# A conditioned decoder block: the gate, attention and state-space projections with tokens on the partitions and 512 weight columns moving

## The chip, the cores and the metric

The kernel runs on one core of one Trainium2 chip. The core has five engines with instruction streams of their own: TensorE (PE), VectorE (DVE), ScalarE (ACT), GpSimd (POOL) and SyncE (SP), which issues the large loads. The metric is the device time of one execution in microseconds.

## The reference

One decoder block for 256 tokens of width 2048, in float32. An input projection `h @ w_in` of the normed, conditioned input gives the state-space input u (1024 columns), q, k and v (1024 each) and two gates (2048 each). Attention and a state-space branch run beside each other and are merged under the gates:

```python
attn = moba_attention(q, k, v, rel_bias)          # 8 heads of 128, causal
ssm = s5_branch(u, ...)                           # scan over tokens, gelu, then y * sigmoid(y @ w_glu + b)
m = sigmoid(gate_a) * (ssm @ w_proj_ssm) + sigmoid(gate_b) * (attn @ w_proj_attn)
x = x + mod * (m @ w_out)
x = x + mod * (squared_relu(h2 @ w_ff1) @ w_ff2)  # d_ff = 8192, then a last norm
```

The modulations come from c through `w_ada`. (The names in this excerpt are shortened.)

## The kernel before, in words

All weights stream once through the core as 439 units of 128x1024 (512 KB). For each unit SP issues a load into `wraw` (seven buffers), ACT casts it to `whi` (L144), DVE forms the rest `wlo = wraw - whi` (L146), and PE multiplies: three products make one product in nearly full precision (activation high times weight high, low times high, high times low). `whi` and `wlo` have four buffers each.

Two forms of multiplication use a unit. `gemm_t` (lines 188 to 190) holds a 128x128 block of the weights still and moves 256 tokens of the activations: 24 matmuls of 256 columns, and the result has output features on partitions and tokens along the row. `gemm_n` (lines 315, 317, 319) holds a 128x128 block of the activations still and moves 512 columns of the weights: 12 matmuls, and the result has tokens on partitions and features along the row. Both write four PSUM banks of 128x512, one accumulation over all k-tiles of the contraction.

In the order of the program: the first units of the input projection, among them ten k-tiles of the first gate columns; the other input units, with six more gate k-tiles; three runs of 16 gate units (i = 1, 2, 3), with attention and then the scan of the state-space branch beside them; `proj_attn` in two halves of eight units (columns cg 0 and 1) with the eight units of `w_glu` between; `proj_ssm` in two halves; `w_out` in two halves; the two MLP products. Before, the gates, `proj_attn`, `w_glu` and `proj_ssm` use `gemm_t`; v, `w_out` and the MLP's first product use `gemm_n`.

Work beside the stream is emitted in lanes: a lane is a list of jobs with a rate, and after each unit `step` adds the rate to a credit and emits jobs while the credit is at least one; `flush` emits what is left. The attention jobs are in lane "m" with rate 1.5, and from the middle of run i=1 that lane holds the scan's jobs `bgl` with rate 0.43. Lane "ada" holds jobs that multiply and reduce a modulation's weights on DVE (L374); they share the `wraw` buffers. A scheduler then sorts each engine's instructions by its own priorities, so the emitted order is not the final one.

The gates live in `ga` (slot X16; x is loaded into the same slot later) and `gb` (slot S1). The merge is in the loop over cg at lines 1188 to 1195: gate times projection (L1193, which also undoes a permutation of the tokens by four), plus the attention part (L1194), and a split of the sum into `mh` and `ml` for `w_out`. Attention keeps scratch rows `asc` in a part of `ga` that is not yet written by the gates. `vr`, `vi` and `ys` are the small matmuls on both sides of the scan.

## Time and profile before

| what | value |
|---|---|
| median of 3 runs | 1403.4 us (1403.07 to 1407.36) |
| the profiled execution, first to last instruction | 1403.3 us |
| PE busy, matmuls | 1369.2 us, 9282 |
| DVE busy, instructions | 1040.4 us, 1474 |
| ACT busy, instructions | 737.7 us, 1004 |
| POOL busy, instructions | 40.9 us, 94 |
| read from HBM | 347.27 MB, 249 GB/s over the span |
| granted TensorE clock, mean | 0.996 |

Busy time of an engine is the union of its instructions' times; matmuls overlap one another, so a matmul's printed duration is longer than the distance between two starts. The chain that ended last is followed back from the last instruction to what released each step. A group's row gives line, engine, operation, output and inputs, count, busy us and mean ns of one, and the idle time ahead with what ended it.

### The profile page before, as it was taken

The numbers are of one execution on the slowest core, as the hardware profiler recorded it, in microseconds if no ns is written. First come the engines' busy times: TensorE is split into PE (matmuls) and PEld (weight loads), VectorE is DVE, ScalarE is ACT, GpSimd is POOL, SyncE is SP. The second block draws the span as 40 slices with busy tenths as digits, with TensorE's granted clock in tenths as the row PEclk, the third lists the DMA queues.
The fourth block names the chain that finished last, engine by engine and source line by source line (L and its number), as shares of the span: only waits on it lengthen the run. The fifth ranks groups of instructions, "written<-read, shape, count | busy, mean of one in ns | idle before, by whom it ended". The sixth has DMA issues, their size and how long they took to land.

```text
span 1403.3 us, 23470 instructions
## 1 busy us (share of the span) xinstructions
PE 1369.2 (98%) x9282; PEld 1219.2 (87%) x9282; DVE 1040.4 (74%) x1474; ACT 737.7 (53%) x1004; POOL 40.9 (3%) x94
## 2 busy tenths in 40 slices
PE   7889999999999999999999999999999999999997
PEld 5779899989999999988888888888888888888885
DVE  5788899776898888977777775777676555554676
ACT  4464565577545853446555554544463553635543
POOL 1000000410001300000000000000000000000000
PEclk9999999999999999999999999999999999999998
DMA  9999996885567988887588777778777566565551
GB/s 352 361 395 332 336 324 221 231 272 205 175 212 236 314 325 301 301 332 291 175 300 282 216 244 246 242 251 276 250 249 235 192 195 190 186 194 187 181 204 60
DMA packets 113293, 353.19 MB, mean 252 GB/s; under 512 B 12080, under 2 KB 12096, under 8 KB 113056
## 3 DMA queue, kind: packets, MB, share of 16 engines
q1 hardware_dynamic: 110096, 346.61, 72.1%
q0 software_dynamic: 2800, 4.58, 1.3%
q8 instruction: 72, 1.18, 0.3%
q10 hardware_dynamic: 288, 0.52, 0.1%
q14 instruction: 37, 0.30, 0.1%
HBM read 347.27 MB, written 2.29 MB: 249 GB/s over the span
## 4 chain that ended last, share of the span: by engine, by line
PE 86%; DMA 7%; DVE 4%; ACT 2%; issue 1%; DVEq 0%; SPq 0%; ACTq 0%
PE pw L216 15%; PE pn L315 9%; PE pn L317 9%; PE pn L319 9%; PE pt L188 8%; PE pt L190 8%; PE pt L189 8%; PE pw L218 8%; DMA wraw<-in_w_in_dram 5%; DVE wlo L146 2%; PE pn L246 2%; PE pn L247 2%; PE pn L248 2%; DVE wraw L374 1%; ACT whi L144 1%
## 5 line engine op out<-in xcount | busy, mean ns | idle before, releaser
L146 DVE TENSOR_TENSOR wlo<-wraw,whi 128x1024 fp32r<-128x1024 f32 x439 | 535.8, 1223 | 276.6 <-ACT whi L144 275.3
L144 ACT CAST whi<-wraw 128x1024 fp32r<-128x1024 f32 x439 | 460.5, 1051 | 531.7 <-PE pn L317 167.8
L216 PE MATMUL pw<-mh,whi 128*128 128x512 f32 x896 | 314.5, 397 | 0.0
L188 PE MATMUL pt<-ah,whi 128*128 128x256 f32 x896 | 251.9, 288 | 5.9 <-ACT whi L144 3.8
L189 PE MATMUL pt<-ah,whi 128*128 128x256 f32 x896 | 249.5, 284 | 0.0
L218 PE MATMUL pw<-mh,wlo 128*128 128x256 f32 x896 | 249.2, 281 | 0.0
L190 PE MATMUL pt<-ah,wlo 128*128 128x256 f32 x896 | 239.7, 286 | 1.4 <-DVE wlo L146 1.1
L374 DVE SCALAR_TENSOR_TENSOR wraw<-wraw,cb 128x1024 f32<-128x1024 f32 x176 | 213.5, 1219 | 0.0
L216 PEld LDWEIGHTS pw<-mh,whi 128*128 128x128 f32 x896 | 167.9, 188 | 39.5
L317 PE MATMUL pn<-whi,ff 128*128 128x512 f32 x480 | 187.0, 390 | 0.0
L315 PE MATMUL pn<-whi,ff 128*128 128x512 f32 x480 | 186.9, 389 | 0.0
L319 PE MATMUL pn<-wlo,ff 128*128 128x512 f32 x480 | 185.8, 389 | 0.0
L188 PEld LDWEIGHTS pt<-ah,whi 128*128 128x128 f32 x896 | 171.6, 192 | 10.3 <-ACT whi L144 5.4
L189 PEld LDWEIGHTS pt<-ah,whi 128*128 128x128 f32 x896 | 172.1, 192 | 0.4 <-DVE ah L146 0.2
L218 PEld LDWEIGHTS pw<-mh,wlo 128*128 128x128 f32 x896 | 169.1, 189 | 1.0
L190 PEld LDWEIGHTS pt<-ah,wlo 128*128 128x128 f32 x896 | 165.0, 192 | 3.8 <-DVE wlo L146 3.4
L315 PEld LDWEIGHTS pn<-whi,ff 128*128 128x128 f32 x480 | 90.1, 188 | 19.0
L319 PEld LDWEIGHTS pn<-wlo,ff 128*128 128x128 f32 x480 | 90.1, 188 | 18.7
L317 PEld LDWEIGHTS pn<-whi,ff 128*128 128x128 f32 x480 | 90.1, 188 | 18.5
L1354 DVE TENSOR_TENSOR y<-y,pn 128x512 f32<-128x512 f32 x48 | 31.0, 684 | 14.6 <-PE pn L319 14.6
L315 PE MATMUL pn<-whi,mh 128*128 128x512 f32 x96 | 37.7, 393 | 1.7 <-ACT whi L144 1.7
L317 PE MATMUL pn<-whi,mh 128*128 128x512 f32 x96 | 37.4, 389 | 0.0
(422 smaller groups left out, 1737.4 us busy)
## 6 DMA issues: line engine op xcount, KB each, us to landing
wraw<-in_w_ff_dram SPq DMA_DIRECT2D x256, 512.0 KB, 4.3
wraw<-in_wat_dram SPq DMA_DIRECT2D x176, 512.0 KB, 5.7
wraw<-in_w_in_dram SPq DMA_DIRECT2D x128, 512.0 KB, 5.5
wraw<-in_w_out_dram SPq DMA_DIRECT2D x32, 512.0 KB, 6.3
wraw<-in_wan_dram SPq DMA_DIRECT2D x16, 512.0 KB, 8.7
wraw<-in_w_proj_attn_dram SPq DMA_DIRECT2D x16, 512.0 KB, 6.5
wraw<-in_w_proj_ssm_dram SPq DMA_DIRECT2D x16, 512.0 KB, 6.7
wraw<-in_w_glu_dram SPq DMA_DIRECT2D x8, 512.0 KB, 5.7
```

The source lines that it names most:

```text
L144: h = self.nc.scalar.copy(hi, src)
L146: s = self.nc.vector.tensor_sub(lo, src, hi.bitcast(F32))
L188: nc.tensor.matmul(o, hi[:, c], xh[:, kx, :], start=st, stop=False, skip_group_check=True)
L189: nc.tensor.matmul(o, hi[:, c], xl[:, kx, :], start=False, stop=False, skip_group_check=True)
L190: self.mm = nc.tensor.matmul(o, lo[:, c], xh[:, kx, :], start=False, stop=sp, skip_group_check=True)
L216: nc.tensor.matmul(banks[b], hi[:, c], x2[:, k0 + k].rearrange("p h s -> p (h s)"), start=i + k == 0, stop=False, skip_group_check=True)
L218: self.mm = nc.tensor.matmul(banks[b][:, 0:S], lo[:, c], x2[:, k0 + k, 0, :], start=False, stop=i == n - 1 and k == 1, skip_group_check=True)
L315: nc.tensor.matmul(o, xh[:, kx, tk], hi[:, c], start=q == 0 and not seeds, stop=False, skip_group_check=bool(seeds))
L317: nc.tensor.matmul(o, xl[:, kx, tk], hi[:, c], start=False, stop=False, skip_group_check=bool(seeds))
L319: self.mm = last = nc.tensor.matmul(o, xh[:, kx, tk], lo[:, c], start=False, stop=q == n - 1, skip_group_check=bool(seeds))
L374: v.scalar_tensor_tensor(w, w, 1.0, self.cb[:, (i % 2) * 1024:(i % 2 + 1) * 1024], op0=OP.mult, op1=OP.mult, accum_out=pc[:, i:i + 1])
L1354: v.tensor_add(d, d, banks[b])
```

## The change

The 96 units of the gates, `proj_attn` and `proj_ssm` go from `gemm_t` to `gemm_n`; `w_glu` stays. `gemm_n` gets the hook `mid` that `gemm_t` had. `ga`, `gb` and the partial gate `gp` now hold tokens on partitions, [P, half of the columns, half of the tokens, 1024], and attention's scratch is the second half of `ga`, columns 0 to 767. The tokens' permutation is now undone where the gated state-space output `gg` is split (the view `nat`), so the multiply of the merge is plain. The contraction of `w_out` needs features on partitions, so the merged rows are transposed on PE: `merged`, eight jobs of four 128x128 transposes into one PSUM tile `trm`, in a lane "tr" of rate 0.75 that starts at credit -1. The jobs of cg 0 run beside the units of `proj_ssm` cg 1, those of cg 1 beside the first half of the units of `w_out`'s first half. The split into `mh` and `ml` then reads PSUM.

```diff
@@ -294,12 +294,14 @@
             then.append((o, c))
         yield then
 
-    def gemm_n(self, src, kts, c0, xh, xl, koff=0, tail=1, seeds=None):
+    def gemm_n(self, src, kts, c0, xh, xl, koff=0, tail=1, seeds=None, mid=None):
         nc = self.nc
         banks = self.seeded("pn", seeds)
         n = len(kts)
         held, prev = [], None
         for i, unit in enumerate(self.stream(src, kts, c0)):
+            if mid and i == n // 2:
+                mid()
             u = (i,) + unit
             held.append(u)
             for t in range(2):
@@ -1024,11 +1026,11 @@
 
         def g_home(part):
             if part and "p" not in gpart:
-                gpart["p"] = self.slot("S4", [P, 8, S], name="gp")
+                gpart["p"] = self.slot("S4", [P, 2, 1024], name="gp")
             if not part:
-                self.ga = self.slot("X16", [P, KT, S], name="ga")
-            t = gpart["p"] if part else self.ga
-            return [(t[:, 2 * b:2 * b + 2, :], pair) for b in range(4)]
+                self.ga = self.slot("X16", [P, 2, 2, 1024], name="ga")
+            t = gpart["p"] if part else self.ga[:, 0]
+            return [(t[:, b // 2, (b % 2) * 512:(b % 2 + 1) * 512], lambda p: p) for b in range(4)]
 
         gpart = {}
 
@@ -1066,8 +1068,8 @@
             home = {0: lambda: qk_home(0), 1: lambda: qk_home(1), 2: v_home, 3: u_home, 4: lambda: g_home(True)}[which]
             old = home() if g0 else None
             c0 = (1024, 2048, 3072, 0, 4096)[which]
-            if which == 2:
-                banks = self.gemm_n(win, kts, c0, self.ah, self.al, seeds=old)
+            if which in (2, 4):
+                banks = self.gemm_n(win, kts, c0, self.ah, self.al, seeds=old, mid=mid)
             else:
                 banks = self.gemm_t(win, kts, c0, self.ah, self.al, mid=mid, seeds=old)
             evac(g_home(False) if which == 4 and g0 else home(), banks)
@@ -1107,9 +1109,9 @@
         qkvu(2, 2, 2)
         self.flush("tab")
         ga = self.ga
-        self.asc = ga[:, 8:14, :].rearrange("p k s -> p (k s)").rearrange("p (i n) -> p i n", i=2)
+        self.asc = ga[:, 1, :, 0:768]
         self.yatt = self.slot("T", [P, 8, S], name="yatt")
-        gb = self.slot("S1", [P, KT, S], name="gb")
+        gb = self.slot("S1", [P, 2, 2, 1024], name="gb")
         def scan(b):
             self.ssm_scan(b)
 
@@ -1139,15 +1141,14 @@
             if i == 3:
                 self.lanes["ada"][1] = RS2
             dst, c0 = ((ga, 4096), (ga, 5120), (gb, 6144), (gb, 7168))[i]
-            banks = self.gemm_t(win, range(KT), c0, self.ah, self.al, mid=to_ssm if i == 1 else None)
+            banks = self.gemm_n(win, range(KT), c0, self.ah, self.al, mid=to_ssm if i == 1 else None)
             for b in range(4):
-                nc.scalar.copy(dst[:, (i % 2) * 8 + 2 * b:(i % 2) * 8 + 2 * b + 2, :],
-                               banks[b].rearrange("p (k s) -> p k s", s=S))
+                nc.scalar.copy(dst[:, i % 2, b // 2, (b % 2) * 512:(b % 2 + 1) * 512], banks[b])
         self.flush("m")
         self.lanes["ada"][1] = RPA
 
         def sig(t, q):
-            d = t[:, 4 * q:4 * q + 4, :].rearrange("p k s -> p (k s)")
+            d = t[:, q // 2, q % 2]
             with self.after(self.done[-1][1]):
                 nc.scalar.activation(d, d, AF.Sigmoid)
 
@@ -1157,9 +1158,9 @@
         for k in range(4):
             self.split(yh[:, 2 * k:2 * k + 2], yl[:, 2 * k:2 * k + 2], self.yatt[:, 2 * k:2 * k + 2])
         def proj_attn(cg):
-            banks = self.gemm_t(a["w_proj_attn"][0], range(8), cg * 1024, yh, yl)
+            banks = self.gemm_n(a["w_proj_attn"][0], range(8), cg * 1024, yh, yl)
             for b in range(4):
-                d = gb[:, cg * 8 + 2 * b:cg * 8 + 2 * b + 2, :].rearrange("p k s -> p (k s)")
+                d = gb[:, cg, b // 2, (b % 2) * 512:(b % 2 + 1) * 512]
                 v.tensor_mul(d, d, banks[b])
 
         proj_attn(0)
@@ -1180,19 +1181,29 @@
                                      bias=self.bglu[:, 2 * b + k:2 * b + k + 1])
             s = slice(2 * b, 2 * b + 2)
             v.tensor_mul(sc4(t), sc4(t), yT[:, s])
-            self.split(gg[:, 0, s], gg[:, 1, s], t)
+            nat = lambda z: z.rearrange("p k (c s) -> p k s c", s=4)
+            self.split(nat(gg[:, 0, s]), nat(gg[:, 1, s]), sc4(t))
         proj_attn(1)
         self.a2("mh")
         mh, ml = self.ah, self.al
+        def merged(cg, t, c):
+            p = self.aux("trm")
+            for k in range(4):
+                nc.tensor.transpose(p[:, k * P:(k + 1) * P], ga[:, cg, t, c * 512 + k * P:c * 512 + (k + 1) * P],
+                                    self.ident)
+            ks, tk = slice(cg * 8 + 4 * c, cg * 8 + 4 * c + 4), slice(t * P, (t + 1) * P)
+            self.split(mh[:, ks, tk], ml[:, ks, tk], p.rearrange("p (k s) -> p k s", s=P))
+
         for cg in range(2):
-            banks = self.gemm_t(a["w_proj_ssm"][0], range(8), cg * 1024, gg[:, 0], gg[:, 1])
+            banks = self.gemm_n(a["w_proj_ssm"][0], range(8), cg * 1024, gg[:, 0], gg[:, 1])
             for b in range(4):
-                s = slice(cg * 8 + 2 * b, cg * 8 + 2 * b + 2)
-                d = ga[:, s, :]
-                dk = d.rearrange("p k (c s) -> p k s c", s=4)
-                v.tensor_mul(dk, dk, banks[b].rearrange("p (k s c) -> p k s c", k=2, s=4))
-                v.tensor_add(d, d, gb[:, s, :])
-                self.split(mh[:, s], ml[:, s], d)
+                c = slice((b % 2) * 512, (b % 2 + 1) * 512)
+                d = ga[:, cg, b // 2, c]
+                v.tensor_mul(d, d, banks[b])
+                v.tensor_add(d, d, gb[:, cg, b // 2, c])
+            if cg:
+                self.flush("tr")
+            self.lane("tr", [lambda cg=cg, t=t, c=c: merged(cg, t, c) for c in range(2) for t in range(2)], .75, -1.0)
         self.lane("x", self.load_x(), .25, -.5)
         self.lane("g1", [lambda ch=ch: g1_row(ch) for ch in range(4)], .25)
         self.lanes["ada"][1] = RWO
@@ -1208,7 +1219,7 @@
                                     turns=((), ((KT - 3, 1),)))
                 banks = next(parts)
             else:
-                banks = self.gemm_n(a["w_out"][0], range(KT), cg * 1024, mh, ml)
+                banks = self.gemm_n(a["w_out"][0], range(KT), cg * 1024, mh, ml, mid=lambda: self.flush("tr"))
             self.flush("x", "g1")
 
             def add1(t):
```

In the order of instructions three places show it. First PE, in gate run i=2. `ah` is the high part of the activations, `pt` and `pn` are the PSUM banks. Before, half a unit is:

```order
L188 MATMUL pt_4176<-ah,whi 128x256
L189 MATMUL pt_4176<-ah,whi 128x256
L190 MATMUL pt_4176<-ah,wlo 128x256
L188 MATMUL pt_4176<-ah,whi 128x256
L189 MATMUL pt_4176<-ah,whi 128x256
L190 MATMUL pt_4176<-ah,wlo 128x256
L188 MATMUL pt_4177<-ah,whi 128x256
L189 MATMUL pt_4177<-ah,whi 128x256
L190 MATMUL pt_4177<-ah,wlo 128x256
L188 MATMUL pt_4177<-ah,whi 128x256
L189 MATMUL pt_4177<-ah,whi 128x256
L190 MATMUL pt_4177<-ah,wlo 128x256
```

After, one whole unit is:

```order
L317 MATMUL pn_3790<-whi,ah 128x512
L319 MATMUL pn_3790<-whi,ah 128x512
L317 MATMUL pn_3791<-whi,ah 128x512
L319 MATMUL pn_3791<-whi,ah 128x512
L317 MATMUL pn_3792<-whi,ah 128x512
L319 MATMUL pn_3792<-whi,ah 128x512
L317 MATMUL pn_3793<-whi,ah 128x512
L319 MATMUL pn_3793<-whi,ah 128x512
L321 MATMUL pn_3790<-wlo,ah 128x512
L321 MATMUL pn_3791<-wlo,ah 128x512
L321 MATMUL pn_3792<-wlo,ah 128x512
L321 MATMUL pn_3793<-wlo,ah 128x512
```

A unit has half as many matmuls, each twice as wide, and in this unit all four that read `wlo` stand behind the eight that read `whi`; before, each third matmul reads `wlo`.

Second DVE, beside the same run i=2, where the scan's rows are (`rw`, `sri`, `tbl`: the scan's rows, its output and its table of powers; the scans are the L881 rows, L883 after). Before:

```order
L146 TENSOR_TENSOR wlo<-wraw,whi 128x1024
L872 TENSOR_TENSOR rw<-vi,tbl 128x512
L881 SCALAR_TENSOR_TENSOR rw<-rw 128x512
L374 SCALAR_TENSOR_TENSOR wraw,pc<-wraw,cb 128x1024
L873 TENSOR_TENSOR rw<-rw 128x512
L146 TENSOR_TENSOR wlo<-wraw,whi 128x1024
L885 TENSOR_TENSOR sri<-rw,tbl 128x8x63
L888 TENSOR_TENSOR sri<-rw,tbl 128x8x63
L881 SCALAR_TENSOR_TENSOR rw<-rw 128x512
L886 TENSOR_TENSOR rw<-rw,tbl 128x8x63
L866 TENSOR_TENSOR rw<-cone,mag_308 128x512
L887 TENSOR_TENSOR sri<-sri,rw 128x8x63
```

After, from the `wlo` of the last unit of run i=2 on:

```order
L146 TENSOR_TENSOR wlo<-wraw,whi 128x1024
L874 TENSOR_TENSOR rw<-vi,tbl 128x512
L883 SCALAR_TENSOR_TENSOR rw<-rw 128x512
L875 TENSOR_TENSOR rw<-rw 128x512
L887 TENSOR_TENSOR sri<-rw,tbl 128x8x63
L890 TENSOR_TENSOR sri<-rw,tbl 128x8x63
L883 SCALAR_TENSOR_TENSOR rw<-rw 128x512
L888 TENSOR_TENSOR rw<-rw,tbl 128x8x63
L868 TENSOR_TENSOR rw<-cone,mag_308 128x512
L870 TENSOR_TENSOR rw<-vr,tbl 128x512
L889 TENSOR_TENSOR sri<-sri,rw 128x8x63
L829 TENSOR_TENSOR tbl<-cvec,g 128x512
```

Between two `wlo` stand at most eight other rows before; after, 19 rows of the scan follow that `wlo` without another, of which eleven are shown.

Third DVE at the merge of cg 0 (`gc` is a small row of a modulation). Before:

```order
L1193 TENSOR_TENSOR ga<-ga,pt_6465 128x2x4x64
L1044 TENSOR_TENSOR gc<-pcs,cols 128x4
L146 TENSOR_TENSOR wlo<-wraw,whi 128x1024
L374 SCALAR_TENSOR_TENSOR wraw,pc<-wraw,cb 128x1024
L1193 TENSOR_TENSOR ga<-ga,pt_6466 128x2x4x64
L1194 TENSOR_TENSOR ga<-ga,gb 128x512
L1193 TENSOR_TENSOR ga<-ga,pt_6467 128x2x4x64
L1193 TENSOR_TENSOR ga<-ga,pt_6468 128x2x4x64
L146 TENSOR_TENSOR wlo<-wraw,whi 128x1024
L1194 TENSOR_TENSOR ga<-ga,gb 128x512 x2
L146 TENSOR_TENSOR mh<-ga,mh 128x2x256
L1194 TENSOR_TENSOR ga<-ga,gb 128x512
```

After:

```order
L1202 TENSOR_TENSOR ga<-ga,pn_5505 128x512
L1202 TENSOR_TENSOR ga<-ga,pn_5506 128x512
L146 TENSOR_TENSOR wlo<-wraw,whi 128x1024
L1202 TENSOR_TENSOR ga<-ga,pn_5507 128x512
L376 SCALAR_TENSOR_TENSOR wraw,pc<-wraw,cb 128x1024
L1202 TENSOR_TENSOR ga<-ga,pn_5508 128x512
L1046 TENSOR_TENSOR gc<-pcs,cols 128x4
L1203 TENSOR_TENSOR ga<-ga,gb 128x512 x2
L146 TENSOR_TENSOR wlo<-wraw,whi 128x1024
L1203 TENSOR_TENSOR ga<-ga,gb 128x512 x2
L146 TENSOR_TENSOR wlo<-wraw,whi 128x1024
L376 SCALAR_TENSOR_TENSOR wraw,pc<-wraw,cb 128x1024
```

The multiply is plain now, and the subtraction for `mh` no longer follows the add: it stands behind the transposes, three `wlo` further on. On SP the order of loads is the same but for x, whose loads stand some five units of `w_out` later; POOL's order is the same.

## The prediction

> **What bounds the kernel now.** I read the page's busy times first, then the shares of the chain that ended last, then the busy time of each engine by stage.
>
> ```profile
> span 1403.3 us, 23470 instructions
> ...
> PE 1369.2 (98%) x9282; PEld 1219.2 (87%) x9282; DVE 1040.4 (74%) x1474; ACT 737.7 (53%) x1004; POOL 40.9 (3%) x94
> ...
> PE 86%; DMA 7%; DVE 4%; ACT 2%; issue 1%; DVEq 0%; SPq 0%; ACTq 0%
> ```
>
> PE is busy for 98% of the span and holds 86% of the chain, so an instruction taken from PE shortens the run wherever PE has no idle time. The windows tell where that is. The gate units lie at 92 to 122 us (ten), 212 to 234 us (six) and 300 to 472 us (48); the 40 units of the projections, 32 of them changed, lie at 472 to 588 us.
>
> ```profile
> core 0: us, PE busy (x) PEld busy (x) DVE busy (x) ACT busy (x) POOL busy (x), PEclk, DMA share, GB/s
> 0.00:178.00 178.00, 156.28 (x1138) 138.52 (x1138) 137.32 (x266) 91.90 (x129) 5.32 (x21) 0.99 0.96 356
> 178.00:300.00 122.00, 121.81 (x1306) 116.60 (x1307) 103.62 (x143) 72.87 (x110) 19.67 (x40) 1.00 0.79 252
> 300.00:360.00 60.00, 59.99 (x523) 58.53 (x522) 41.04 (x76) 40.80 (x81) 0.00 (x0) 1.00 0.68 236
> 360.00:417.00 57.00, 57.00 (x707) 56.26 (x706) 55.25 (x72) 29.26 (x36) 0.00 (x0) 1.00 0.57 182
> 417.00:472.00 55.00, 55.00 (x653) 54.33 (x650) 47.61 (x68) 31.48 (x40) 15.33 (x32) 1.00 0.78 254
> 472.00:588.00 116.00, 114.30 (x951) 114.01 (x950) 101.28 (x137) 57.60 (x71) 0.00 (x0) 1.00 0.87 310
> ...
> 634.00:1403.00 769.00, 758.85 (x3803) 642.50 (x3801) 515.66 (x670) 392.23 (x518) 0.58 (x1) 1.00 0.67 220
> ```
>
> Up to 178 us the DMA engines are busy for 0.96 of the time and PE idles 21.7 us: transfers bound that stretch, and a cheaper unit gains nothing in it. From 178 to 588 us PE idles 1.9 us in all. There PE is the bound, with VectorE (DVE) close behind at one place: 55.25 of 57 us in 360 to 417, where the scan of the state-space branch runs beside the third run of gate units (i=2). The granted clock is 1.00 throughout, so it needs no term.
>
> **The unit.** A unit is one weight tile of 128x1024. Before, it is 24 matmuls of 256 columns; after, 12 of 512. Matmuls are pipelined, so the price is the pitch of starts, not the printed duration.
>
> ```profile
> 194.61 0.28 PE L188 MATMUL pt<-ah,whi 128*128 128x256 f32 x1
> ...
> 195.81 0.28 PE L189 MATMUL pt<-ah,whi 128*128 128x256 f32 x1
> ...
> 1145.81 0.39 PE L319 MATMUL pn<-wlo,ff 128*128 128x512 f32 x1
> ...
> 1147.17 0.39 PE L319 MATMUL pn<-wlo,ff 128*128 128x512 f32 x1
> ```
>
> Ten steps from 194.61 to 195.81 are 0.120 us each, a unit 24 x 0.120 = 2.88. Six steps from 1145.81 to 1147.17 are 0.2267 each, a unit 12 x 0.2267 = 2.72. The saving is 0.16 us a unit. Of 96 changed units ten stand in the transfer-bound stretch and save 0; 86 x 0.16 = **-13.8 us**. The Trainium skill, "TensorE: Matmul & The Clock Gate", section "Back-to-back issue gap", gives an isolated warm gap of N/2.4 + 2.5 ns: 109.2 ns at 256 columns and 215.8 at 512. By that a unit would go from 2.62 to 2.59 and 86 units would save some 2.6 us as an estimate, not 13.8; the trace's 0.120 and 0.2267 differ from it, the narrow form more, and the measurement decides.
>
> **The transposes.** Thirty-two PE transposes of 128x128 are new. The nearest row is a run of twelve at the seam of the MLP, in the chain (start, length, engine, what); below it stands a group of the page (busy us, mean ns of one, idle before):
>
> ```profile
> 356.89 1.08 PE vr L864 x32
> 357.97 0.93 PE vi L864 x32
> ...
> 380.25 0.38 PE ys L902 x8
> ...
> 821.15 1.31 PE trf L1296 x12
> ...
> L773 PE MATMUL ptr<-ident,ga 128*128 128x128 f32 x24 | 4.7, 272 | 0.0
> ```
>
> 1.31/12 = 0.109, so 32 cost **+3.5 us**, all on PE while it is the bound. If each group of four also broke the stream the cost could approach a printed single transpose (0.272, the last row): 32 x 0.272 = 8.7 at most; 3.5 is the low end too. The results go from PSUM through the same eight ACT casts and eight DVE subtractions as before. The last group is issued one unit (2.72) before w_out needs it; a cast, a subtraction and a weight row ahead of each in its queue may take some 3.6 by the rows shown next and the weight subtraction's 1.22, so 0 to 0.9 may show; I take 0.
>
> ```profile
> L774 ACT COPY ga<-ptr 128x384 f32<-128x384 f32 x8 | 3.8, 469 | 2.1 <-PE ptr L773 2.1
> L146 DVE TENSOR_TENSOR gg<-sg,gg 128x512 fp32r<-128x512 f32 x4 | 2.6, 684 | 0.0
> L1193 DVE TENSOR_TENSOR ga<-ga,pt 128x512 f32<-128x512 f32 x8 | 8.7, 1106 | 0.0
> L1194 DVE TENSOR_TENSOR ga<-ga,gb 128x512 f32<-128x512 f32 x8 | 5.3, 700 | 0.0
> L1144 ACT COPY ga<-pt 128x512 f32<-128x512 f32 x4 | 2.3, 584 | 2.3 <-PE pt L190 2.1
> ```
>
> **The merge.** The permuted multiply costs 1106 ns; the plain one after should cost what the plain add of the same size does, 700: 8 x 0.41 = 3.2 us less on DVE. Here DVE is on the chain, in order of time:
>
> ```profile
> 573.49 0.68 DVE ga L1194
> 574.18 0.42 DVE mh L146
> 574.70 1.22 DVE wlo L146
> 576.06 0.91 issue
> 577.09 6.31 DMA wraw<-in_w_out_dram
> 583.50 1.05 ACT whi L144
> 584.60 0.50 PE pn L315
> ...
> PE pn L315 <- ACT whi L144: 1.7, 1, 1.7
> ```
>
> The wait at its end, 1.7 us, is the only PE idle time between 472 and 588 us (116 - 114.30). Merge rows late on DVE held the weight tile that the load of w_out needs. With 3.2 us less ahead of that load, **-1.7 us**; between 0 and -1.7, since no more idle is there to take. In exchange the permutation moves to four casts and four subtractions of gg, DVE 684 now and at most 1106: 4 x 0.42 = 1.7 us, under PE work at 101.28 busy of 116; taken as 0. The load of x moves some five w_out units later on SP, with the transfers of two to three units for cover; 0. POOL's order stays, and the gate copies on ACT keep their number and shapes.
>
> **What moves on DVE.** A unit's matmuls are now emitted in one or two blocks of rows, and the scheduler puts other engines' rows elsewhere. Before, scan rows and weight subtractions (wlo) alternate, at most eight rows between two wlo. After, the order has 19 scan rows (16 elementwise, 3 scans) in one piece between the wlo of the last i=2 unit and the first i=3 unit. PE drinks one wlo per 2.72 us, and a pile delays it. The pitch of DVE rows, from the stretch where it is full:
>
> ```profile
> 381.29 1.21 DVE L881 TENSOR_TENSOR_SCAN rw<-rw 128x512 f32<-128x512 f32 x1
> 382.42 1.20 DVE L374 SCALAR_TENSOR_TENSOR wraw<-wraw,cb 128x1024 f32<-128x1024 f32 x1
> ...
> 384.15 1.22 DVE L146 TENSOR_TENSOR wlo<-wraw,whi 128x1024 fp32r<-128x1024 f32 x1
> 385.28 0.68 DVE L885 TENSOR_TENSOR sri<-rw,tbl 128x504 f32<-128x504 f32 x1
> 385.88 0.68 DVE L888 TENSOR_TENSOR sri<-rw,tbl 128x504 f32<-128x504 f32 x1
> ```
>
> A scan or 1024-wide row takes 1.13 (381.29 to 382.42, 384.15 to 385.28), a 512-wide row 0.60. From the wlo of that last unit to the wlo ten units later the order holds 34 rows of 512 and 23 long ones: 34 x 0.60 + 23 x 1.13 = 46.4 us. PE's work over the same ten units is 27.2, two runs of 64 small matmuls ys at 0.38 for eight (2 x 3.04) and vr with vi (2.0): 35.3. DVE is 11.1 short, which its lead must pay. wlo has four buffers, so DVE can lead by about three units of PE plus the small matmuls ahead: 3 x 2.72 + 3.04 + 2.0 - 1.13 = 12.1. Full lead gives 0; no lead gives 11.1. Before, DVE had 55.25 of 57 full in the window and PE no idle, so a lead existed, and around the pile the new order reads wlo after eight of a unit's twelve matmuls (8 x 0.2267 = 1.8 us in) where before it was read after two (0.24). Both put me nearer the full-lead end; but the queues that feed the lead are full too. I take a third: **+4 us**, range 1 to 9.
>
> One more wait is new: the gate copies now land where attention's last two heads keep scratch, so they wait for those heads. The copies' price is 4 x 0.584 = 2.3, the upper end; the lower end is 0. I take **+1**.
>
> **Sum.** 1403.3 - 13.8 + 3.5 - 1.7 + 4 + 1 = **1396.3 us**. The profiled span is 1403.3 and the median of the runs 1403.4, so no offset is needed.
>
> **Rivals.**
>
> *No stall* (DVE's lead is whole, and attention's scratch is free in time): 1403.3 - 13.8 + 3.5 - 1.7 = 1391.3. For it: PE had no idle beside a DVE that was 97% full. Against: the 19-row pile is new.
>
> *Stalls eat the gain*: DVE rows take their printed lengths (0.68, 1.22) instead of their pitch, as rows that wait on each other do: 34 x 0.68 + 23 x 1.22 = 51.2, short by 15.9; half of the lead, 6.0, leaves 9.9. Then 1391.3 + 9.9 + 1 = 1402.2, no measurable change.
>
> *Slower*: the pile starts with no lead, because the units before it are themselves fed late: the 15.9 just worked out, plus 1 for attention: 1391.3 + 16.9 = 1408.2. It decides, against the run before, once the stalls pass 12.0 us. Against it is the full PE row of 360 to 417.
>
> *The unit is not cheaper*: if columns alone set the price, 12 x 2 x 0.120 = 2.88 and nothing is saved: 1403.3 + 3.5 - 1.7 + 5 = 1410.1. Against it stands the direct pitch of the same form, 0.2267. By the Trainium skill's gap above, in the same section, the time would be 1403.3 - 2.6 + 3.5 - 1.7 + 5 = 1407.5, an estimate on this rival's side; the trace's pitch speaks against it.
>
> **How the numbers follow.** Forecast 0.46, no stall 0.20, eaten 0.20, slower 0.10, unit not cheaper 0.04. A measurement of this kernel tells about 0.3%, 4.2 us, from no change, so faster means under 1399.2 and slower over 1407.6. The forecast's own range, from 1393 to 1401, has some 0.40 under 1399.2 and 0.06 above; with no stall's 0.20 and 0.02 of the eaten case faster is 0.62. Same is 0.06 and 0.18 plus 0.03 of the slower case, 0.27; slower 0.11. The range goes from 1390.5 (a little under no stall) to 1405, which leaves out the slower cases and the best corner of no stall.
>
> **What would show it.** A unit of gates at 2.72 us on PE, 12 starts apart by 0.227; 32 transposes at 0.11; the multiply of the merge near 0.70; no wait of PE at the start of w_out. In the third run of gates, i=3, PE idle time behind wlo of 1 to 9 us, at the pile, and short waits of ACT's gate copies after attention. I am wrong if PE idles more than 12 us there, if the pitch is 0.24, or if the stages after 588 us move.

## The result, and the profile after

The change makes the kernel slower: 1413.5 us median of four runs (1411.95 to 1414.33) against 1404.3, ratio 1.0059 (95% interval 1.0046 to 1.0072), which is 6.5 to 10.1 us. The forecast was 1396.3. The profiled execution spans 1411.0 us, 7.7 more than the one of before.

Busy times and the shares of the chain that ended last, from the page of the changed kernel:

```profile
span 1411.0 us, 21226 instructions
...
PE 1367.1 (97%) x8162; PEld 1162.4 (82%) x8162; DVE 1037.9 (74%) x1474; ACT 736.7 (52%) x1004; POOL 40.9 (3%) x94
...
PE 80%; DMA 8%; DVE 8%; ACT 2%; issue 2%; DVEq 0%; SPq 0%; ACTq 0%
```

PE has 1120 instructions fewer, but its share of the chain falls from 86 to 80%, and DVE's rises from 4 to 8%. The windows of the changed kernel (us of each engine, then granted clock, DMA share and GB/s) show where:

```profile
300.00:411.00 111.00, 111.00 (x840) 92.72 (x840) 86.09 (x133) 67.04 (x115) 0.00 (x0) 1.00 0.59 200
411.00:456.00 45.00, 40.88 (x390) 33.73 (x389) 42.71 (x61) 20.06 (x27) 3.82 (x8) 0.96 0.76 251
456.00:534.00 78.00, 76.03 (x425) 66.29 (x424) 66.84 (x89) 49.69 (x61) 11.53 (x24) 1.00 0.86 297
534.00:560.00 26.00, 23.03 (x85) 17.14 (x84) 17.96 (x26) 7.42 (x8) 0.00 (x0) 0.87 0.75 275
560.00:612.00 52.00, 50.00 (x231) 40.08 (x230) 46.82 (x66) 21.61 (x25) 0.00 (x0) 1.00 0.84 292
```

Before, PE idled 1.9 us between 178 and 588 us, and none in two of these stretches:

```profile
411.00:456.00 45.00, 45.00 (x633) 44.20 (x632) 39.12 (x55) 23.17 (x31) 4.52 (x10) 1.00 0.75 247
...
534.00:560.00 26.00, 26.00 (x219) 26.00 (x218) 20.90 (x26) 8.39 (x8) 0.00 (x0) 1.00 0.91 321
```

Now it idles 4.1 us in the third gate run (411 to 456), 2.0 in the next 78 us, 3.0 around the start of `proj_ssm` (534 to 560) and 2.0 in the 52 us after. In two of these stretches the granted clock, 1.00 before, is 0.96 and 0.87. The rows that answer to the terms of the forecast are as forecast. Starts of gate matmuls, and the transposes in the chain:

```profile
439.87 0.39 PE L317 MATMUL pn<-whi,ah 128*128 128x512 f32 x1
...
441.91 0.39 PE L317 MATMUL pn<-whi,ah 128*128 128x512 f32 x1
...
604.26 0.44 PE trm L1192 x4
```

Nine steps take 2.04 us, 0.227 each; four transposes take 0.44, 0.11 each. And the groups by shape (busy us, mean ns):

```profile
L1202 DVE TENSOR_TENSOR ga<-ga,pn 128x512 f32<-128x512 f32 x8 | 5.1, 676 | 0.0
L146 DVE TENSOR_TENSOR gg<-sg,gg 128x512 fp32r<-128x512 f32 x4 | 4.3, 1128 | 0.0
L144 ACT CAST gg<-sg 128x512 fp32r<-128x512 f32 x4 | 4.2, 1168 | 0.0
```

The multiply of the merge costs 676 ns (1106 before), and the permutation that moved to gg costs 1128 where it was 684.

To see where the time goes, I took from the timeline of PE when the last matmul of a unit ends, and compared with the same unit of the kernel before, both counted from unit 79, the last ahead of the gate runs. Minus is earlier. e1 and so on are the experiments below; the last line would read about -11 if only the terms of the forecast without stalls acted (80 units at -0.16, +3.5, -1.7).

| unit (what ends there) | changed | e1 | e2 | e5 | e13 | e17 |
|---|---|---|---|---|---|---|
| 112 (start of gate run i=3) | -4.7 | -4.3 | 0.7 | -3.9 | -4.3 | -4.4 |
| 123 (after the pile of scan rows) | 0.0 | -1.1 | 0.7 | -0.7 | -5.9 | -6.0 |
| 135 (`proj_attn` 0) | -1.9 | -0.2 | -0.3 | -1.4 | -7.8 | -7.7 |
| 143 (`w_glu`) | 0.1 | -0.2 | 1.0 | -1.8 | -8.0 | -8.4 |
| 151 (`proj_attn` 1) | -0.5 | -0.2 | -0.3 | -3.1 | -9.3 | -9.6 |
| 159 (`proj_ssm` 0) | 5.4 | -0.2 | 4.4 | -4.3 | -10.4 | -10.9 |
| 167 (`proj_ssm` 1) | 5.1 | 0.4 | 3.5 | -6.1 | -12.1 | -12.2 |
| 183 (`w_out` 0) | 8.8 | 2.8 | 6.5 | -3.7 | -9.7 | -9.8 |
| 230 (MLP) | 8.8 | 3.1 | 6.6 | -2.2 | -9.2 | -10.0 |

The changed kernel gains 4.7 us in 33 units, as summed, loses all of it beside the scan, gains again, and then loses 2.0 in `w_glu` and 5.9 in the first eight units of `proj_ssm`. The loss of 3.7 from 167 to 183 holds the transposes of the second half. From there on nothing changes.

The waits in the first of the two places, 411 to 456 us, and in the second, 534 to 560 us (us in total, times, longest):

```profile
PE ys L904 <- DVE sri L892: 2.1, 1, 2.1
PE pn L321 <- DVE wlo L146: 2.1, 1, 2.1
...
ACT whi L144 <- DMA wraw<-in_w_proj_ssm_dram: 10.6, 5, 3.4
ACT whi L144 <- PE pn L319: 8.3, 1, 8.3
PE pn L317 <- ACT whi L144: 2.4, 3, 1.1
PE pn L321 <- DVE wlo L146: 0.5, 1, 0.5
```

In the first place PE waits for DVE twice: once for a wlo behind the scan's rows, once for the scan's own output. In the second it waits for casts that wait for loads. The chain tells what the loads waited for:

```profile
527.49 1.27 DVE wlo L146
528.77 1.15 DVE wraw L376 x2
529.94 5.06 DMA wraw<-in_w_proj_ssm_dram
535.10 1.06 ACT whi L144
536.19 1.24 DVE wlo L146
537.44 6.46 DMA wraw<-in_w_proj_ssm_dram
544.00 1.05 ACT whi L144
545.10 0.79 PE pn L317
```

A load starts when DVE has let go of one of the seven `wraw` buffers, by a wlo or by a modulation row (L376). Release, transfer of 5 to 6.5 us, cast and wlo, release: DVE and the transfers stand in one ring. PE's order takes the first bank of four units before the other banks of the first, so at the start of a product it needs four new weights within 3 us; with no lead it waits for each.

### The profile page after: what moved, and what is told of

It reads as the page before. It is cut to its first block, busy times and chain, and to the rows that moved or that the text cites. A ratio compares the mean times of both kernels' runs of the same rounds, so it can differ in the third digit from the quotient of the medians.

```text
span 1411.0 us, 21226 instructions
## 1 busy us (share of the span) xinstructions
PE 1367.1 (97%) x8162; PEld 1162.4 (82%) x8162; DVE 1037.9 (74%) x1474; ACT 736.7 (52%) x1004; POOL 40.9 (3%) x94
## 4 chain that ended last, share of the span: by engine, by line
PE 80%; DMA 8%; DVE 8%; ACT 2%; issue 2%; DVEq 0%; SPq 0%; ACTq 0%
PE pw L216 15%; PE pn L317 13%; PE pn L319 13%; PE pn L321 13%; PE pw L218 8%; DMA wraw<-in_w_in_dram 4%; PE pt L188 3%; PE pt L190 3%; PE pt L189 3%; DVE wlo L146 3%; DVE wraw L376 2%; PE pn L246 2%; PE pn L248 2%; PE pn L247 2%; ACT whi L144 1%
## 5 line engine op out<-in xcount | busy, mean ns | idle before, releaser
L376 DVE SCALAR_TENSOR_TENSOR wraw<-wraw,cb 128x1024 f32<-128x1024 f32 x176 | 213.5, 1219 | 0.0
L317 PE MATMUL pn<-whi,ah 128*128 128x512 f32 x320 | 126.7, 398 | 6.4 <-ACT whi L144 6.4
L319 PE MATMUL pn<-whi,ah 128*128 128x512 f32 x320 | 124.9, 392 | 0.0
L321 PE MATMUL pn<-wlo,ah 128*128 128x512 f32 x320 | 110.6, 394 | 3.0 <-DVE wlo L146 3.0
L188 PE MATMUL pt<-ah,whi 128*128 128x256 f32 x384 | 106.6, 289 | 4.7 <-ACT whi L144 2.6
L189 PE MATMUL pt<-ah,whi 128*128 128x256 f32 x384 | 106.5, 286 | 0.0
L190 PE MATMUL pt<-ah,wlo 128*128 128x256 f32 x384 | 98.7, 287 | 0.3
L188 PEld LDWEIGHTS pt<-ah,whi 128*128 128x128 f32 x384 | 73.5, 192 | 7.8 <-ACT whi L144 3.9
L317 PEld LDWEIGHTS pn<-whi,ah 128*128 128x128 f32 x320 | 60.1, 188 | 22.1 <-ACT whi L144 9.2
L189 PEld LDWEIGHTS pt<-ah,whi 128*128 128x128 f32 x384 | 74.3, 194 | 0.5 <-DVE ah L146 0.4
```

The lines of the kernel that those rows point to most:

```text
L188: nc.tensor.matmul(o, hi[:, c], xh[:, kx, :], start=st, stop=False, skip_group_check=True)
L189: nc.tensor.matmul(o, hi[:, c], xl[:, kx, :], start=False, stop=False, skip_group_check=True)
L190: self.mm = nc.tensor.matmul(o, lo[:, c], xh[:, kx, :], start=False, stop=sp, skip_group_check=True)
L317: nc.tensor.matmul(o, xh[:, kx, tk], hi[:, c], start=q == 0 and not seeds, stop=False, skip_group_check=bool(seeds))
L319: nc.tensor.matmul(o, xl[:, kx, tk], hi[:, c], start=False, stop=False, skip_group_check=bool(seeds))
L321: self.mm = last = nc.tensor.matmul(o, xh[:, kx, tk], lo[:, c], start=False, stop=q == n - 1, skip_group_check=bool(seeds))
```

## Experiments

All ratios are against the kernel before, run beside; the changed kernel is 1.0059. A ratio of 0.001 is 1.4 us.

**e1: projections back**, and with them the plain split of gg (its lines are left out here). The projections' products then have the other layout than the gates.

```diff
-            banks = self.gemm_n(a["w_proj_attn"][0], range(8), cg * 1024, yh, yl)
+            banks = self.gemm_t(a["w_proj_attn"][0], range(8), cg * 1024, yh, yl)
-            banks = self.gemm_n(a["w_proj_ssm"][0], range(8), cg * 1024, gg[:, 0], gg[:, 1])
+            banks = self.gemm_t(a["w_proj_ssm"][0], range(8), cg * 1024, gg[:, 0], gg[:, 1])
```

> The changed kernel, but proj_attn and proj_ssm go back to 256 token columns moving (gg split plainly again); gates, transposes and the plain merge stay. The products then stand in the other layout than the gates, so this is for its time only. Theory A (the faster projections outrun their weights): the projection stage comes back to the pace of before, which loses the 32 x 0.16 = 5.1 us of cheaper units but wins back the some 9 us that the trace shows lost at the starts of w_glu and proj_ssm: about 1408 (1405 to 1410), against 1412.6 for the changed kernel. Rival B (the transposes and the merge seam cost it): nothing is won back and 5.1 us are lost, 1417.

1406.1 us, ratio 1.0011 (1.0002 to 1.0021): 6.7 us less than the changed kernel, though its 32 units are dearer. In 534 to 560 us PE is full again:

```profile
534.00:560.00 26.00, 26.00 (x219) 26.00 (x218) 20.54 (x29) 9.32 (x9) 0.00 (x0) 1.00 0.91 332
```

Theory A held: the cheaper projection units cost more than they save. The plain split of gg is a small part of this at most, as e4 shows.

**e2: gates back.**

```diff
-            banks = self.gemm_n(win, range(KT), c0, self.ah, self.al, mid=to_ssm if i == 1 else None)
+            banks = self.gemm_t(win, range(KT), c0, self.ah, self.al, mid=to_ssm if i == 1 else None)
```

(and the first gate units in the same way.)

> The changed kernel, but the 64 gate units go back to 256 token columns moving; projections, transposes and merge stay. For its time only, since the layouts differ. Theory A (the pile of scan rows in the third gate run stalls PE): 54 x 0.16 = 8.6 us of cheaper units are lost, the some 6.5 us of stall and slow clock in the third run are won back: about 1414.5 (1412 to 1417). Rival (the pile is there in any case, the units set the rest): 1421.

1412.1 us, 1.0057 (1.0045 to 1.0069): no difference from the changed kernel. What the gates save they lose beside the scan, and with the old gates PE is full there:

```profile
411.00:456.00 45.00, 45.00 (x633) 44.20 (x632) 39.11 (x56) 22.70 (x30) 6.02 (x13) 1.00 0.76 252
```

**e3: no transposes.** The split reads the rows of `ga` as they lie.

```diff
-            p = self.aux("trm")
-            for k in range(4):
-                nc.tensor.transpose(p[:, k * P:(k + 1) * P], ga[:, cg, t, c * 512 + k * P:c * 512 + (k + 1) * P],
-                                    self.ident)
+            p = ga[:, cg, t, c * 512:(c + 1) * 512]
```

> The changed kernel without the 32 transposes: the split for w_out reads the merged rows directly, so w_out gets its rows untransposed. By their price of 0.109 us each on a full PE: 3.5 us less, 1409. Rival B (the transposes hold up the start of w_out and its weights): 6 us less or more, 1406 or below. If they hide in PE's idle time: 1412 to 1413.

1408.1 us, 1.0029 (1.0016 to 1.0043): 4.2 us less, give or take 2.6, which fits their price of 3.5. Rival B's 6 us lie within the error and are not excluded, and in the traces some of it shows: at unit 167 e3 is no earlier than the changed kernel (4.8 us against 5.1), and it gains everything from there to unit 183, 3.8 us where 16 transposes cost 1.8. The transposes of the first half stand in time that PE loses anyway.

**e4: gg split plainly.**

```diff
-            nat = lambda z: z.rearrange("p k (c s) -> p k s c", s=4)
-            self.split(nat(gg[:, 0, s]), nat(gg[:, 1, s]), sc4(t))
+            self.split(gg[:, 0, s], gg[:, 1, s], t)
```

> The changed kernel with the split of gg plain again (tokens stay permuted in the state-space half of the merge). In the trace of the changed kernel this split takes 1128 ns on DVE where it took 684, four times, and 1168 on ACT: 1.8 us of DVE time just before proj_ssm, whose weights come late. Theory A1 (that delay is passed on through the weight buffers to PE): 1 to 3 us less, 1410 to 1411.5. Rival (DVE has slack there, the loads alone bound it): no change, 1412 to 1413.

1411.7 us, 1.0051 (1.0038 to 1.0063). That is about 1 us less, and the intervals overlap, so between theory A1 and no effect it is not settled. It is not the main cause.

The next edits change rates. RSS is the rate of the scan's jobs. The others are rates of lane "ada", the modulation tiles: R3 ahead of the gate runs, RS0 from their start to the middle of run i=1, RS1 from there to the end of i=2, RS2 in i=3, RPA beside the projections, RWO beside `w_out`.

**e5: ten modulation tiles out of the projection stage.**

```diff
-RS0 = .7
+RS0 = 1.6
-RPA = .75
+RPA = .5
```

> The changed kernel with two numbers of the ada lane changed: RS0 from .7 to 1.6 and RPA from .75 to .5, so that ten of the 30 modulation tiles that are loaded and reduced between the 40 projection units are taken elsewhere (six of them ahead, into gate run i=1). The scan stays as it is. Theory A (in the projection stage loads and DVE rows of the ada lane leave the faster units without lead): the 7 us at the start of proj_ssm and most of the 2 us at w_glu come back, about 1406 (1404 to 1408) where the changed kernel is at 1413. Rival (the order of PE's rows at the start of a product alone makes the stall, whatever the feed): 1412 or more.

1402.3 us, 0.998 (0.9972 to 0.9989): 11 us less, more than expected. The two stalls of the projections are gone, and part of that of the scan stays:

```profile
411.00:456.00 45.00, 42.26 (x463) 34.90 (x459) 43.44 (x60) 22.06 (x30) 3.83 (x8) 0.96 0.73 241
...
534.00:560.00 26.00, 26.00 (x116) 21.56 (x115) 20.70 (x27) 9.49 (x10) 0.00 (x0) 1.00 0.89 321
```

The rival is not excluded by this run alone: the scheduler, which sees fewer rows, also lets PE take the first bank of three units ahead of the other banks there, not of four. e10 settles it.

**e6: scan rows spread.**

```diff
-RS1 = .25
+RS1 = 0.0
-RSS = .43
+RSS = .36
```

> The changed kernel with RSS from .43 to .36 and RS1 from .25 to 0: in the order of DVE the other rows ahead of the first i=3 wlo fall from 11.4 us to none and the longest such piece from 11.4 to 6, and no ada rows stand in gate run i=2. The projection stage keeps its 30 ada tiles. Theory A (the pile of scan rows stalls PE in run i=3): PE has no idle time there and keeps its clock, 5 to 6.5 us less than the changed kernel, about 1407. Rival (the scan's own chain of dependences sets the pace, not the pile): 1412 or more.

1410.4 us, 1.0036 (1.0024 to 1.0048): 3 us less where 6 were expected. The stall in the third gate run is gone, and a new one stands where the slower scan is needed, ahead of `w_glu`:

```profile
411.00:456.00 45.00, 45.00 (x416) 37.33 (x415) 44.09 (x60) 18.87 (x20) 0.00 (x0) 1.00 0.79 262
472.00:491.00 19.00, 16.29 (x72) 13.14 (x70) 16.53 (x22) 12.76 (x15) 8.60 (x18) 0.98 0.91 295
491.00:534.00 43.00, 39.35 (x252) 36.73 (x253) 34.83 (x49) 21.12 (x28) 0.00 (x0) 0.89 0.73 256
```

Both theories were too simple: the pile can be spread, but the scan has a due time.

**e7 and e8: both edits together, on the changed kernel and on the kernel before.**

```diff
-RS0 = .7
-RS1 = .25
-RSS = .43
-RPA = .75
+RS0 = 1.6
+RS1 = 0.0
+RSS = .36
+RPA = .5
```

> The changed kernel with both: RSS .36, RS1 0, RS0 1.6, RPA .5. If the two stalls are separate places and all of the loss: 1413 - 7 - 6 = 1400 (1398 to 1403), which is faster than the kernel before. If one stall moves to the other place: 1406.

> The kernel before with the same four numbers, as a control. Theory A: before, both places have lead enough and PE is full, so the numbers bring nothing, 1403 to 1405. Rival (the numbers are worth as much in any layout): 1395 or less.

e7: 1410.5 us, 1.0041 (1.0028 to 1.0053); e8: 1412.2 us, 1.0051 (1.0036 to 1.0066). Both missed. The late scan costs either kernel time at `w_glu`, and the modulation rows put off by RS1 come in one lot beside the MLP: in e7 PE idles 2.3 us there.

```profile
760.00:780.00 20.00, 17.75 (x91) 15.04 (x91) 19.18 (x37) 6.89 (x12) 0.00 (x0) 0.91 0.92 329
```

**e9: short modulation rows in the projection stage**, loads whole. `thin` is set from the end of the gate runs to the start of `w_out` (these lines are left out here and in e10).

```diff
+                m = P if self.thin else 1024
-                v.scalar_tensor_tensor(w, w, 1.0, self.cb[:, (i % 2) * 1024:(i % 2 + 1) * 1024], op0=OP.mult,
-                                       op1=OP.mult, accum_out=pc[:, i:i + 1])
+                v.scalar_tensor_tensor(w[:, 0:m], w[:, 0:m], 1.0, self.cb[:, (i % 2) * 1024:(i % 2) * 1024 + m],
+                                       op0=OP.mult, op1=OP.mult, accum_out=pc[:, i:i + 1])
```

> The changed kernel with its own numbers, but the 30 modulation rows that DVE reduces between the projection units read 128 columns instead of 1024; their loads stay whole. The modulations are wrong by that, so this is for its time. It takes 30 x 1.0 = 30 us of DVE time out of the projection stage and no byte. Theory A-DVE (wlo and the release of weight buffers come late because DVE is full): the stalls at w_glu and proj_ssm go, 8 to 10 us less than the changed kernel, about 1403 to 1405. Theory A-DMA (the 30 extra tiles of 512 KB on the queue make the weights late): 0 to 3 us less, 1410 to 1413.

**e10: short loads in the projection stage**, rows 896 wide from what was loaded (the lines of the rows are left out).

```diff
+            m = P if self.thin else 1024
-                ld = nc.sync.dma_start(w, self.a["wat"][r0:r0 + P, (i % 2) * 1024:(i % 2 + 1) * 1024])
+                ld = nc.sync.dma_start(w[:, 0:m], self.a["wat"][r0:r0 + P, (i % 2) * 1024:(i % 2) * 1024 + m])
```

> The changed kernel with its own numbers, but the 30 modulation tiles of the projection stage load 128 columns (64 KB) instead of 1024 (512 KB), and DVE still makes a row of 896 columns of each. For its time. It takes 30 x 448 KB = 13.8 MB off the queue, 38 us of transfers at 358 GB/s, and 4 us of DVE time. Theory A-DMA: the stalls go, 1403 to 1405. Theory A-DVE: 0 to 3 us less, 1410 to 1413. If both are needed: each gives about half.

e9: 1401.8 us, 0.9985 (0.9975 to 0.9995); e10: 1403.6, 0.9992 (0.9983 to 1.0001). Each alone takes away nearly the whole stall, 10.4 and 9.4 us less than the changed kernel. So neither "DVE" nor "transfers" is the answer: both stand in the ring of buffers, and relief in either gives the lead back. In e10 the first 30 matmuls of `proj_ssm` stand in the very order of the changed kernel, four units for the first bank, and PE hardly waits: that order needs a lead, and alone it makes no stall. In e9, as in e5, it is three units. The two ways are seen in the windows of e9 and of e10:

```profile
534.00:560.00 26.00, 25.21 (x111) 20.38 (x110) 16.42 (x31) 10.16 (x10) 0.00 (x0) 1.00 0.97 337
```

```profile
534.00:560.00 26.00, 25.62 (x112) 20.45 (x111) 22.42 (x34) 9.57 (x10) 0.00 (x0) 1.00 0.64 206
```

**e11: e5 with a faster scan** (RSS .43 to .5).

```diff
-RSS = .43
+RSS = .5
```

> The version with moved ada tiles (RS0 1.6, RPA .5: 1402.3) and RSS from .43 to .5, RS1 as it was: the other DVE rows beside units 96 to 127 fall as 14.4, 19.0, 18.4, 12.6 us by eight units where they were 10.9, 8.8, 28.0, 16.2; the longest piece is 9.1 instead of 11.4, and the scan ends no later. Theory A: the 2.7 us of idle PE and the some 1.5 us of slow clock in the third gate run go, 1398 to 1400. Rival (the first piece of 9.1 now stalls run i=2): 1402 or more.

1406.7 us, 1.0009 (0.9999 to 1.0018). The rival held: the pile came earlier, into run i=2, and PE idles there.

```profile
300.00:411.00 111.00, 107.08 (x820) 88.73 (x819) 91.91 (x148) 64.54 (x110) 0.00 (x0) 1.00 0.66 228
411.00:456.00 45.00, 42.47 (x403) 34.92 (x402) 43.35 (x61) 22.92 (x31) 7.66 (x16) 1.00 0.72 224
```

**e12: the control of e5**, its two numbers on the kernel before.

```diff
-RS0 = .7
+RS0 = 1.6
-RPA = .75
+RPA = .5
```

> The kernel before with RS0 1.6 and RPA .5 alone, the control for the moved ada tiles. Theory A: the wider units needed the lead, the old ones had it: PE was full there but for 1.7 us at the merge, so 1402 to 1405. Rival (the two numbers help any layout): 1395.

1403.7 us, 0.9989 (0.998 to 0.9998). The numbers bring the old kernel 1.5 us and the changed one 11. The wider units needed the lead, the old ones had it.

**e13: short modulation rows from the middle of run i=1 to the end of the projections**, 47 of them.

```diff
             self.lanes["ada"][1] = RS1
+            self.thin = True
```

> The changed kernel, but all 47 modulation rows from the middle of gate run i=1 to the end of the projections read 128 columns instead of 1024; loads stay whole. For its time. It adds the 17 rows beside the scan to the 30 of the run with thin rows (1401.8). Theory (DVE is short of time in the scan, 11 us or so on paper; with 17 us less it is not): the 4.7 us lost from unit 112 to 123 and the 1.5 us after them come back, 1396 to 1397, near the time that my sum gives without stalls and with 4 us of transposes. Rival (the scan's chain of dependences stalls PE whatever else DVE does): 1401.

1394.0 us, 0.9921 (0.9909 to 0.9933): the lowest of all, and near the 1391.3 of the sum without stalls. The scan's chain of dependences is as it was, so it does not make the stall; DVE's time and the places that its rows get by it do (with shorter rows the scheduler also spreads the pile, the longest piece between two `wlo` from 19 rows to 11, so the two are not told apart). PE is full where it idled:

```profile
411.00:456.00 45.00, 45.00 (x417) 37.62 (x418) 37.22 (x63) 25.64 (x33) 11.02 (x23) 1.00 0.82 278
456.00:534.00 78.00, 78.00 (x434) 68.19 (x433) 51.11 (x96) 47.64 (x57) 4.34 (x9) 1.00 0.94 338
534.00:560.00 26.00, 26.00 (x116) 21.46 (x115) 17.77 (x34) 9.48 (x10) 0.00 (x0) 1.00 0.93 343
```

**e14 to e16: all rows kept, placed elsewhere.** e14, and e16 on the kernel before; e15 has 2.4, 0, .35, .6, .75 in the same order.

```diff
-RS0 = .7
-RS1 = .25
-RS2 = .7
-RPA = .75
-RWO = .5
+RS0 = 2.8
+RS1 = 0.0
+RS2 = .35
+RPA = .55
+RWO = .7
```

> The changed kernel with the ada lane moved further: RS0 2.8, RS1 0, RS2 .35, RPA .55, RWO .7, RSS as it was. Other DVE rows by eight units from 104 on: 17.4, 11.8, 13.8 us where the version with moved tiles had 8.8, 28.0, 16.2, the longest piece 5.4; three ada tiles more per eight units stay out of the third gate run, four to five stand by eight projection units. Theory: no stall in the scan, and a lead at proj_ssm, 1396 to 1399, faster than both. Rival (18 ada tiles in the first eight units of run i=1 delay attention and its gates): 1402 or more.

> The same with RS0 2.4, RS1 0, RS2 .35, RPA .6, RWO .75: 17 tiles ahead, five by eight projection units, six by eight units of w_out, none left over for the MLP. 1397 to 1400 by the theory; if five tiles by eight projection units are already too many, the stall at proj_ssm comes back and it lies 3 us above the run with RPA .55.

> The kernel before with RS0 2.8, RS1 0, RS2 .35, RPA .55, RWO .7, as the control: with no stall to remove, 1402 to 1405. Rival (the numbers help any layout): 1398.

e14: 1403.3 us, 0.9994 (0.9985 to 1.0003); e15: 1403.1, 0.9983 (0.9973 to 0.9992); e16: 1414.6, 1.0072 (1.0059 to 1.0086). The rival of e14 held, e15 lies above its range too, and the control e16 is 10 us slower where no change was expected. The scan and the projections run without a stall in e14, but 17 or 18 tiles in eight units are too many for the start of run i=1, in either layout. Of e14:

```profile
300.00:411.00 111.00, 105.34 (x719) 85.77 (x718) 92.98 (x149) 64.34 (x107) 0.00 (x0) 0.98 0.69 236
411.00:456.00 45.00, 45.00 (x500) 37.83 (x499) 37.99 (x52) 23.84 (x32) 6.55 (x14) 1.00 0.66 205
```

**e17 and e18: some tiles ahead of the gate runs.** e17 as below; e18 has R3 .8 and RS0 1.2. Between units 56 and 79 stand 17 tiles in e17 and 19 in e18, where there were 12.

```diff
-R3 = .5
-RS0 = .7
-RS1 = .25
-RS2 = .7
-RPA = .75
-RWO = .5
+R3 = .7
+RS0 = 1.6
+RS1 = 0.0
+RS2 = .35
+RPA = .55
+RWO = .75
```

> The changed kernel with the ada tiles moved to where both DVE and loads have room: R3 .7 (22 to 17 of them ahead of the gate runs, between units 56 and 79), RS0 1.6 (12 at run i=1, the number that did no harm), RS1 0, RS2 .35, RPA .55, RWO .75. DVE rows in the scan as in the run with 2.4. If the stall at the start of run i=1 there (9 us) came from 17 to 18 tiles in eight units and is gone with 12: 1395 to 1398, faster than the kernel before by .5% or so. If the tiles ahead of unit 79 cost PE time themselves: 1400 or more.

> The same with R3 .8, RS0 1.2 (nine tiles at run i=1, 19 between units 56 and 79): 1395 to 1398 if neither place is full; above the run with R3 .7 if the units 56 to 79 are the tighter place.

e17: 1398.2 us, 0.9955 (0.9943 to 0.9967), faster than the kernel before by 6 us with all work kept, and the best whole version. e18: 1401.5, 0.9976 (0.9965 to 0.9986), above its range. From unit 79 on, e17 gains 10.0 us (the table), like e13; it pays for this ahead of unit 79:

```profile
178.00:300.00 122.00, 116.24 (x1200) 108.33 (x1198) 101.69 (x144) 67.45 (x102) 19.69 (x40) 0.98 0.84 257
```

Why e18 is slower than e17 is not shown: its profiled run, 1398.8 us, happens to be faster than that of e17, 1400.9, and PE idles there less ahead of 300 us (2.5 us against 5.8) and more from 300 to 411 (2.8 against 0.1). The best place of these tiles was not searched further, and the numbers of e17 were not tried on the kernel before, so e17 does not compare the two layouts under the same rates.

## Why the prediction was wrong

**The unit: right.** 0.227 us a step, and 33 gate units gain 3.9 to 4.7 us in the changed kernel, e5, e13 and e17 (5.3 summed). The rule of the Trainium skill, "TensorE: Matmul & The Clock Gate", section "Back-to-back issue gap", by which 86 units would save some 2.6 us, is not borne out, since 33 units alone gain more. Nor is the rival that the unit is not cheaper.

**The transposes: right in price.** 0.11 each in the chain; 4.2 us by e3 against 3.5. That the sum agrees so well is partly luck: the first half cost nothing that shows, and the second more than its price.

**The merge: right in price, not in effect.** The multiply fell to 676 ns. The 1.7 us of idle time were not gained, since casts and weights were by then late for another reason; in e13 and e17 they were: from unit 159 to 167 these gain 1.7 and 1.3 us, where eight cheaper units (1.3) less 16 transposes (1.8) would give a loss of 0.5 without it.

**The scan: right in mechanism, low in size.** +4 was taken, with 1 to 9. From unit 112 to 123 the changed kernel loses 4.7 us where e13 gains 1.6: 6.3. Of that 4.2 are waits, of which only one half is the late wlo of the forecast and the other the scan's own late output. Some 1.5 is the clock: e9 has the same two waits at a granted clock of 1.00 and loses 3.2 us over these units. Of the two reasons given for a lead the second, that wlo is read late in a unit, did not carry far: the next wlo after the pile was in time, but the lead was not won back, and PE stood six units later, at the wlo of unit 118.

**Attention's scratch: nothing.** +1 was taken. PE is busy for 111.00 of 111 us from 300 to 411.

**The step that failed** is the projection stage. Its 32 units stood in the sum with -5.1 us and no charge, and the dearer rows of gg were put "under PE work at 101.28 busy of 116; taken as 0". The mean over 116 us hid that loads, at 310 GB/s of the 356 that the first stretch shows, and DVE, at 0.87 of its time, stand in one ring and are both nearly full there. Faster PE used up the lead: against e13 the stage (units 136 to 167) loses 11.3 us, 2.2 of it in `w_glu`, 7.0 in the first half of `proj_ssm`. e1, e5, e9 and e10 each show it, by giving the lead back in a different way. (The rows of gg took 1128 ns, a little over the 1106 that were their upper bound; by e4 that is the smaller matter.) With it the sum comes out: the 1396.3 of the forecast, 11.3 for the stage and 2.3 more for the scan, less 1 for attention, are 1408.9, against 1411.0 in the profiled run and 1412.6 by the ratio; the rest is not attributed.

**The clock: the sentence "it needs no term" failed too.** It was right for the kernel before, where PE hardly idled; in the changed kernel, stalls brought a term of their own.

**The rivals.** The one that was slower got the place (the scan) and some of the price, but what made the kernel slower was the projections' feed, which no rival named. That its 1408.2 lies near the measured time is luck: it stood for 15.9 us of stall in the scan, where 6.3 were found. The same holds for the 1410.1 and 1407.5 of the dearer units. Nor did the signs of being wrong point at the stage: PE idled 4.1 us in the third gate run, not 12, and the pitch is 0.227; only the part after 588 us moved, by 3.7 us up to unit 183.

## What to carry to other kernels

Before an engine that holds the chain is made faster, look at each stage for how far its weights are ahead at the start of each product, not at the mean busy time of the engines that feed it: two feeders at 87% in one ring of buffers turned a gain of 4 us (units 136 to 167 in e13) into a loss of 7. Then move side work out of the fed stage in the same edit: the same change was 0.6% slower with the old rates and 0.45% faster with new ones, while the numbers of e5 brought the old layout 0.1% (those of e17 were not tried on it). And a place that was filled to relieve another has its own limit, as e11, e14 and e18 show.

## What the runs showed of the hardware

A stall of PE can cost more than its length. After the waits around 540 us the same matmuls start at half the rate. Eight steps here, in the timeline of the changed kernel, take 3.41 us, 0.426 each, where they took 0.227:

```profile
545.69 0.63 PE L319 MATMUL pn<-whi,gg 128*128 128x512 f32 x1
...
549.10 0.53 PE L319 MATMUL pn<-whi,gg 128*128 128x512 f32 x1
...
445.98 0.33 PE L904 MATMUL ys<-sri,cc 64*64 64x64 f32 x4 [2.07 <-DVE sri L892]
```

```profile
545.00:550.00 5.00, 4.91 (x13) 3.91 (x14) 3.42 (x5) 0.04 (x1) 0.00 (x0) 0.56 0.88 347
550.00:555.00 5.00, 5.00 (x24) 4.11 (x23) 0.57 (x1) 1.66 (x2) 0.00 (x0) 1.00 0.25 85
```

The granted clock falls between 542 and 544 us (0.64 there), is 0.56 from 545 to 550 us and 1.00 again after. The ten matmuls from 545.1 to 549.5 lose 2.1 us by it (4.4 less 10 x 0.227), beside the 2.9 us of waits that came before. The Trainium skill, "TensorE: Matmul & The Clock Gate", Part 1, gives 426.7 ns for 512 columns with the array cold, which is what stands here, and puts the fall after an idle window of some 3.4 us. Here no single wait was that long: 1.1, 0.5 and 0.8 us with one or two matmuls between them came before the fall, and at 446 us one of 2.07 (the last row of the first fence) was followed by small matmuls at half rate a microsecond later. The same waits do not always bring it: in e9 and e10 PE stood for 2.07 and 2.08 us at the same two places beside the scan, and the clock stayed at 1.00. This is e9:

```profile
411.00:456.00 45.00, 40.85 (x397) 33.53 (x396) 42.71 (x60) 20.04 (x26) 4.79 (x10) 1.00 0.75 249
```

What decides it is not shown.

Writing float32 with a step of four elements costs: 1128 ns on DVE (where one operand is read with that step too) and 1168 on ACT for 512 columns, where the plain rows took 684 and 622. Modulation rows shortened from 1024 to 128 columns took 289 ns in e9, not an eighth of 1219.
